# One kernel, one change: modulation sums streamed through the array, half a gate moved into the forgetting stage, and a memory projection taken token tile by token tile

## The chip, the cores and the metric

The kernel runs on one core of a Trainium2 chip. The number that counts is the device time of one execution, in microseconds. The kernel before took 1184.94 us (median of three runs, 1183.32 to 1185.14). The execution that was profiled took 1180.89 us, of which its trace spans 1179.1 us.

Names of the engines: PE is TensorE's matrix multiplication and PEld its weight load, DVE is VectorE, ACT is ScalarE, POOL is GpSimd, and SP is the queue that issues most DMAs.

## The reference

Two transformer blocks run one after the other on 512 tokens of 1024 channels. Only the first block's beginning matters here.

```python
mod = silu(c) @ w_ada + b_ada                     # c: 1024, w_ada: 1024 x 3072
shift, scale, gate = split(mod, 3)
h = rms_norm(x, g_pre) * (1 + scale) + shift
qa, ka, va, fa, za, qb, kb, vb, zb = split(h @ w_in, ...)
oa = forgetting_attention(qa, ka, va, fa + b_fgate) * silu(za)      # 8 heads of 64
ob = sliding_window_sink_attention(rope(qb), rope(kb), vb, sinks) * silu(zb)
x = x + gate * rms_norm(concat(oa, ob) @ w_out, g_post)
```

The second block reads a memory of 256 tokens, whose keys and values are `rms_norm(mem) @ w_mem_kv`.

## The kernel before

Most projections are done in a split form: a float32 matrix is cut into a high part (`wh`, `hh`) and a low rest (`wl`, `hl`), and three passes (high by high, high by low, low by high) replace one float32 product. A pass over 512 columns is one matmul. Weights come from memory as `raw` tiles (three buffers); ACT casts the high part, DVE or POOL subtracts for the low part.

**The opening.** `w_ada` for shift and scale is loaded in eight chunks of 1 MB (`load_ada`), five buffers in all. Chunk k gives shift and scale of channels 128k to 128k+127, as two columns. There are two ways to get them. `products(k, act)` and `products(k, dve)` scale the eight slices of the chunk by silu(c) and add them up on ACT and DVE, and `sums(k)` closes with two matmuls that have one column each. `sums_pe(k)` does the whole sum on PE with 16 matmuls of one column, the chunk itself being the stationary operand. Chunks 2, 3 and 5 go through `sums_pe`, the other five through `products`. Then `modulate(k)` adds the bias and `hidden(k)` forms `hh` and `hl` for the 128 channels: one ACT instruction, one on DVE or ACT, and a subtraction on POOL. At the end the `w1c` loop multiplies the eight channel tiles with a 264-column slice of `w_in` (keys and values of the window attention, forget gates): 12 matmuls for each k. All instructions in this part are in the order in which they are written, since `Ordered` pins them (line 345 is that helper, so all of them carry L345).

**Window attention and forgetting attention.** From here on the instructions are ordered by a list scheduler by priority, and what each engine gets is a fixed list. `staged` walks over attention steps in three phases (scores `sc`, transposes `tp`, product with values `pv`) and after each step calls `fill(k)`: the next k pieces of pending projection work, taken from a queue of generators. The window stage has two groups of four query blocks (`swa_sc`, `swa_tp`, `swa_pv`), two pieces for each step. Its queue holds the gates zb0, zb1, za0, za1 (`z_gen`: 48 matmuls each, two tanh, two DVE products) and the first query and key pair qk0. The forgetting stage has 32 steps (four head pairs `pr`, two heads, four query blocks) and one piece for each step. Its queue: `va`, `qk1`, `mv` (`value_row`), `qk2`, `qk3`, `gate` (`gate_row`). A step's scores need DVE to drain them, and there are two score banks, so PE can be two scores ahead of DVE.

`value_row` projects half of the memory's values: 256 tokens, that is two tiles t of 128, in two PSUM banks. For each of four weight quarters q it loads 512 KB of weights (`wv`, two buffers) and 256 KB of the transposed memory (`mT2`, one buffer), and runs 2 x 2 float32 matmuls:

```python
b = wk.tile([P, 2, 256], F32, tag="gb", name="mT2", bufs=1)
nc.sync.dma_start(out=b, in_=mT_d[:, 2 * q:2 * q + 2, :])
nc.sync.dma_start(out=a, in_=A["w_mem"][2][:, 2 * q:2 * q + 2, :])
```

SP issues DMAs in order, and one that waits for a buffer holds all behind it.

The functions that the change touches, with the lines that the profile names:

Of the kernel before, what the change touches and what calls it, by code (L numbers as in the profile page):

```python
# [20 lines left out]
P = 128  # L21
S = 512
NT = 4
KT = 8
# [16 lines left out]
NW = 512  # L41
# [51 lines left out]
def two_block_kernel(ctx: ExitStack, tc: tile.TileContext, A: dict, out: bass.AP):  # L93
    nc = tc.nc
    pe, act, dve, pool = nc.tensor, nc.scalar, nc.vector, nc.gpsimd
    fill = Fill()
# [49 lines left out]
    def mm_tile():  # L146
        return psm.tile([P, 512], F32, tag="mm", name="mm")
# [4 lines left out]
    def tp_tile():  # L152
        return pst.tile([P, 512], F32, tag="tp", name="tp")
# [210 lines left out]
    with ExitStack() as st:  # L364
# [8 lines left out]
        gs = pa1.tile([P, 8], F32, name="gs")  # L373
        mod = pa1.tile([P, 16], F32, name="mod")
# [18 lines left out]
        def squares(x, ss, ts):  # L393
            for t in ts:
                act.activation(out=xt[:, 2 * t:2 * t + 2, :].rearrange("p a b -> p (a b)"), in_=x[:, t, :], func=AF.Square, accum_out=ss[:, t:t + 1])
# [18 lines left out]
        def sums(k):  # L414
            pms[k] = tp_tile() if k in (0, 1, 4, 6) else mm_tile()
            for j in range(2):
                pe.matmul(out=pms[k][:, j:j + 1], lhsT=accs[k][0][:, j * P:(j + 1) * P], rhs=ones[:, 0:1], start=True, stop=True)

        def sums_pe(k):
            pms[k] = tp_tile() if k in (0, 1, 4, 6) else mm_tile()  # L420
            for j in range(2):
                for i in range(KT):
                    pe.matmul(out=pms[k][:, j:j + 1], lhsT=adas[k][:, i, j * P:(j + 1) * P], rhs=cs[:, i:i + 1], start=(i == 0), stop=(i == KT - 1))
# [43 lines left out]
        dve.tensor_copy(out=mrs, in_=rsqrt_small(pa, mss, 2, 1.0 / 1024, 1e-6, "rn2"))  # L467
        squares(xn, xss, range(NT))
# [11 lines left out]
        load_ada(5, 6, 7)  # L480
        sums(1)
        modulate(0)
        hidden(0, dve, pool)
        products(4, act)
        products(4, dve)
        sums_pe(3)
        sums(4)
        modulate(1)
        hidden(1, dve, pool)
        for t in range(2):  # L490
            act.activation(out=mk[:, t, :], in_=kb_[t], func=AF.Copy, scale=mrs[:, t:t + 1])
        modulate(2)
        hidden(2, dve, pool)
        products(6, act)
        products(6, dve)
        sums_pe(5)
        sums(6)
        wr, w = [], {}
        for q in range(4):
            wr.append(wp.tile([P, 2, 264], F32, tag="raw", name="raw", bufs=3))  # L500
            sp.dma_start(out=wr[q], in_=A["w1c"][:, 2 * q:2 * q + 2, :])
            if q == 2:
                break
# [9 lines left out]
        products(7, act)  # L513
        w1c_split(0, dve)
        wr.append(wp.tile([P, 2, 264], F32, tag="raw", name="raw", bufs=3))
        sp.dma_start(out=wr[3], in_=A["w1c"][:, 6:8, :])
        sp.dma_start(out=mT_d, in_=mT)
        modulate(3)
        hidden(3, act, pool)
        w1c_split(1, pool)  # L520
        modulate(4)
        hidden(4, act, pool)
        products(7, dve)
        w1c_split(2, dve)
        modulate(5)
        hidden(5, act, pool)
        w1c_split(3, dve)
        modulate(6)
        hidden(6, act, pool)
        wb = [sc_tile(), sc_tile(), pv_tile(), mm_tile()]  # L530
        for k in range(KT):
            if k == 4:
                sums(7)
                modulate(7)
                hidden(7, dve, dve)
            wh, wl = w[k]
            for t in range(NT):
                for i, (a, b) in enumerate(((hh, wh), (hh, wl), (hl, wh))):
                    pe.matmul(out=wb[t][:, 0:264], lhsT=a[:, k, t * P:(t + 1) * P], rhs=b, start=(k == 0 and i == 0), stop=(k == KT - 1 and i == 2))
# [95 lines left out]
    with ExitStack() as stS:  # L635
# [84 lines left out]
        fill.add("za1", z_gen("za1", 2))  # L720
# [77 lines left out]
        fill.until("za1")  # L798
# [27 lines left out]
    def value_row():  # L826

        banks = [mm_tile() for t in range(2)]
        for q in range(4):
            a = wk.tile([P, 2, NW], F32, tag="wg", name="wv")  # L830
            b = wk.tile([P, 2, 256], F32, tag="gb", name="mT2", bufs=1)
            nc.sync.dma_start(out=b, in_=mT_d[:, 2 * q:2 * q + 2, :])
            nc.sync.dma_start(out=a, in_=A["w_mem"][2][:, 2 * q:2 * q + 2, :])
            for k in range(2):
                for t in range(2):
                    m = pe.matmul(out=banks[t], lhsT=b[:, k, t * P:(t + 1) * P], rhs=a[:, k, :], start=(q + k == 0), stop=(2 * q + k == KT - 1))
                    if t == 0:
                        tie(m)
            if q < 3:
                yield  # L840
        mv = wk.tile([P, 2, NW], F32, tag="csb", name="mv2", bufs=1)
        for t in range(2):
            act.activation(out=mv[:, t, :], in_=banks[t], func=AF.Copy, scale=mrs[:, t:t + 1])
        nc.scalar.dma_start(out=v_d[:, :, 0:NW], in_=mv)
        yield
# [63 lines left out]
    fill.add("qk2", qk_gen(2, fa))  # L909
    fill.add("qk3", qk_gen(3, fb))  # L910
    fill.add("gate", gate_row())
    staged([(pr, m, n) for pr in range(4) for m in range(2) for n in range(NT)], fox_sc, fox_tp, fox_pv, 2, 1)
# [692 lines left out]
```

## Time and profile before

| | |
|---|---|
| median of three runs | 1184.94 us |
| profiled execution | 1180.89 us, span 1179.1 us |
| PE busy | 1151.2 us, 98% of the span |
| DVE busy | 877.5 us, 74% |
| ACT busy | 561.3 us, 48% |
| POOL busy | 194.1 us, 16% |
| moved by DMA | 168.39 MB, mean 143 GB/s |

PE is busy nearly always, so time is made of three things: the PE work there is, the clock at which it runs, and the few places where PE waits. The profile gives the first by its timeline, the second as a granted clock for any stretch (1.00 is full speed), the third as idle time with the releaser beside it.

### The profile page before, as it was taken

What the parts mean: (1) busy time and instruction counts of PE and PEld (TensorE: products, weight loads), DVE (VectorE), ACT (ScalarE), POOL (GpSimd) and SP (SyncE); (2) the same over time, 40 slices, a digit from 0 to 9 for tenths busy, and PEclk for the clock granted to TensorE, in tenths of its full rate; (3) what the DMA queues carried; (4) which work ended last, traced back from release to release, by engine and by line L of the source; (5) the groups of instructions that cost most, each with busy time, mean ns of one, the idle gap of its engine ahead of it and who ended that gap; (6) DMA issues with size and microseconds to landing.
All of it is one profiled execution on the core that took longest, in us unless ns stands there. A gap on an engine that the chain in (4) does not pass through costs nothing. (4 is left out here: it accounts for less than half of the span.)

```text
span 1179.1 us, 16340 instructions
## 1 busy us (share of the span) xinstructions
PE 1151.2 (98%) x5652; PEld 948.0 (80%) x5652; DVE 877.5 (74%) x1876; ACT 561.3 (48%) x1255; POOL 194.1 (16%) x153
## 2 busy tenths in 40 slices
PE   7999999999899999999999999999999999999998
PEld 4978777676688889888888778888888888888887
DVE  5786865666697599999999998999786287554342
ACT  6565754564564544555545544454433236232231
POOL 0441000000022202012020221031111031111000
PEclk9699999999999999999999999999999999999999
DMA  9643223455486332433334334343387455432233
GB/s 379 228 174 111 72 67 106 123 165 177 149 268 200 119 95 83 116 101 115 107 96 112 120 131 134 97 137 125 123 300 238 135 201 177 132 108 90 89 107 107
DMA packets 59905, 168.39 MB, mean 143 GB/s; under 512 B 7120, under 2 KB 10448, under 8 KB 58544
## 3 DMA queue, kind: packets, MB, share of 16 engines
q1 hardware_dynamic: 36544, 124.50, 33.5%
q10 hardware_dynamic: 23280, 42.86, 10.5%
q8 instruction: 44, 0.72, 0.3%
q14 instruction: 37, 0.30, 0.1%
HBM read 138.90 MB, written 21.63 MB: 136 GB/s over the span
## 5 line engine op out<-in xcount | busy, mean ns | idle before, releaser
L170 ACT CAST wh<-raw 128x512 fp32r<-128x512 f32 x352 | 212.6, 620 | 207.4 <-PE mm L202 101.6
L172 DVE TENSOR_TENSOR wl<-raw,wh 128x512 fp32r<-128x512 f32 x264 | 196.2, 755 | 99.7 <-ACT wh L170 98.0
L172 POOL TENSOR_TENSOR wl<-raw,wh 128x512 fp32r<-128x512 f32 x88 | 122.5, 1392 | 823.1 <-ACT wh L170 796.9
L202 PE MATMUL mm<-hh,wh 128*128 128x512 f32 x640 | 252.7, 395 | 0.0
L202 PE MATMUL mm<-hh,wl 128*128 128x512 f32 x640 | 251.3, 393 | 0.0
L202 PE MATMUL mm<-hl,wh 128*128 128x512 f32 x640 | 250.9, 392 | 0.0
L1052 DVE SCALAR_TENSOR_TENSOR cv<-u,vec,cv 128x512 f32<-128x512 f32 x240 | 192.8, 803 | 2.1
L202 PEld LDWEIGHTS mm<-hh,wl 128*128 128x128 f32 x640 | 120.2, 188 | 24.8 <-issue 0.2
L202 PEld LDWEIGHTS mm<-hh,wh 128*128 128x128 f32 x640 | 120.3, 188 | 23.5 <-issue 0.2
L202 PEld LDWEIGHTS mm<-hl,wh 128*128 128x128 f32 x640 | 120.4, 188 | 23.0
L221 PE MATMUL mm<-wh,hh 128*128 128x512 f32 x256 | 101.3, 396 | 0.0
L221 PE MATMUL mm<-wl,hh 128*128 128x512 f32 x256 | 100.9, 394 | 0.0
L221 PE MATMUL mm<-wh,hl 128*128 128x512 f32 x256 | 100.2, 393 | 0.0
L202 PE MATMUL mm<-bh,wh 128*128 128x512 f32 x192 | 75.2, 392 | 0.0
L202 PE MATMUL mm<-bh,wl 128*128 128x512 f32 x192 | 74.7, 389 | 0.0
L202 PE MATMUL mm<-bl,wh 128*128 128x512 f32 x192 | 74.7, 389 | 0.0
L1166 ACT ACTIVATE dp<-dp,dst 128x128 f32<-128x128 f32 (+3 forms) x64 | 35.8, 559 | 50.3 <-DVE dst L1164 49.0
L221 PEld LDWEIGHTS mm<-wh,hl 128*128 128x128 f32 x256 | 48.1, 188 | 9.7
L221 PEld LDWEIGHTS mm<-wh,hh 128*128 128x128 f32 x256 | 48.2, 188 | 9.2
L221 PEld LDWEIGHTS mm<-wl,hh 128*128 128x128 f32 x256 | 48.2, 188 | 8.7
L202 PEld LDWEIGHTS mm<-bl,wh 128*128 128x128 f32 x192 | 36.0, 188 | 7.7 <-issue 0.2
L202 PEld LDWEIGHTS mm<-bh,wh 128*128 128x128 f32 x192 | 36.0, 188 | 7.7 <-issue 0.2
(381 smaller groups left out, 2144.4 us busy)
## 6 DMA issues: line engine op xcount, KB each, us to landing
raw<-in_w_dram SPq DMA_DIRECT2D x88, 512.0 KB, 4.4
raw<-in_w_out_dram SPq DMA_DIRECT2D x24, 512.0 KB, 4.1
raw<-in_w2n_dram SPq DMA_DIRECT2D x24, 512.0 KB, 3.9
ada<-in_w_ada_dram SPq DMA_DIRECT2D x8, 1024.0 KB, 10.2
raw<-in_w1n_dram SPq DMA_DIRECT2D x8, 512.0 KB, 3.6
wg<-in_w_gate_dram SPq DMA_DIRECT2D x8, 512.0 KB
raw<-in_w_mem_dram SPq DMA_DIRECT2D x8, 512.0 KB, 4.3
k<-ks SPq DMA_DIRECT2D x32, 128.0 KB, 3.7
```

Of the source, the lines that this page charges most:

```text
L170: act.copy(out=wh, in_=raw[:, s])
L172: eng.tensor_tensor(out=wl, in0=raw[:, s], in1=f(wh), op=ALU.subtract)
L202: m = pe.matmul(out=ps, lhsT=a[:, c0:c0 + P], rhs=at(b, k), start=(n == 0 and i == 0), stop=(n == KT - 1 and i == 2))
L221: x = pe.matmul(out=ps, lhsT=at(a, k)[:, t * P:(t + 1) * P], rhs=b[:, 0:n], start=(m == 0 and i == 0), stop=(m == KT - 1 and i == 2))
L1052: dve.scalar_tensor_tensor(out=a, in0=u[:, j:j + S], scalar=dw[:, m * 31 + j:m * 31 + j + 1], in1=a, op0=ALU.mult, op1=ALU.add)
L1166: act.activation(out=p_[:, :w], in_=p_[:, :w], func=AF.Exp, scale=-1.0, bias=st_[:, 0, n, m:m + 1], accum_out=st_[:, 1, n, m:m + 1])
```

## The change

1. `sums_pe` no longer uses the chunk as stationary operand with a moving column. A new tile `csr` holds silu(c) repeated over 128 columns and is the stationary operand, and the chunk is streamed past it: 8 matmuls of 256 columns instead of 16 of one. Each row of the result is the same, and `column(k)` picks the diagonal with two fused DVE multiply-and-add instructions. Chunks 6 and 7 now go this way as well (their `products` are gone). The order of loads and of `modulate`/`hidden` is new, four `hidden` calls move a part from ACT to DVE, three move the subtraction from POOL to DVE, and chunks 6 and 7 are summed inside the `w1c` loop.
2. `za1` leaves the window stage's queue and joins the forgetting stage's, after `qk2`. The forgetting stage now takes alternately one and two pieces for each step.
3. `value_row` runs over token tiles on the outside: for each t one 512 KB tile of the transposed memory and all four weight quarters, so that the weights are loaded twice (2 MB more).

```diff
+        csr = pa1.tile([P, KT, P], F32, name="csr")
...
         def sums_pe(k):
-            pms[k] = tp_tile() if k in (0, 1, 4, 6) else mm_tile()
+
+            pms[k] = mm_tile()
+            for i in range(KT):
+                pe.matmul(out=pms[k][:, 0:256], lhsT=csr[:, i, :], rhs=adas[k][:, i, :], start=(i == 0), stop=(i == KT - 1))
+
+        def column(k):
+
+            row, pms[k] = pms[k], pa.tile([P, 2], F32, tag="colk", name="colk")
             for j in range(2):
-                for i in range(KT):
-                    pe.matmul(out=pms[k][:, j:j + 1], lhsT=adas[k][:, i, j * P:(j + 1) * P], rhs=cs[:, i:i + 1], start=(i == 0), stop=(i == KT - 1))
+                t = pa.tile([P, P], F32, tag="colt", name="colt", bufs=1)
+                dve.tensor_tensor_reduce(out=t, in0=row[:, j * P:(j + 1) * P], in1=ident, scale=1.0, scalar=0.0, op0=ALU.mult, op1=ALU.add, accum_out=pms[k][:, j:j + 1])
...
+        dve.tensor_copy(out=csr, in_=cs.unsqueeze(2).to_broadcast([P, KT, P]))
...
         sums(0)
         sums_pe(2)
-        load_ada(5, 6, 7)
         sums(1)
-        modulate(0)
-        hidden(0, dve, pool)
-        products(4, act)
-        products(4, dve)
         sums_pe(3)
-        sums(4)
-        modulate(1)
-        hidden(1, dve, pool)
...
+        load_ada(5)
...
+        for q in range(3):
+            w1c_load(q)
+        load_ada(6, 7)
+        modulate(0)
+        hidden(0, dve, pool)
+        column(2)
+        modulate(2)
+        hidden(2, dve, pool)
+        modulate(1)
+        hidden(1, dve, pool)
+        products(4, act)
+        products(4, dve)
+        sums(4)
+        column(3)
+        modulate(3)
+        hidden(3, dve, pool)
...
+        modulate(4)
+        sums_pe(5)
         w1c_split(0, dve)
+        hidden(4, dve, dve)
...
+        column(5)
+        modulate(5)
+        hidden(5, dve, dve)
...
         for k in range(KT):
-            if k == 4:
-                sums(7)
-                modulate(7)
-                hidden(7, dve, dve)
+            if k in (2, 3):
+                sums_pe(k + 4)
+                column(k + 4)
+                modulate(k + 4)
+                hidden(k + 4, dve, dve)
...
-        fill.add("za1", z_gen("za1", 2))
...
-        fill.until("za1")
+        fill.until("za0")
...
+        for t in range(2):
+            b = wk.tile([P, KT, P], F32, tag="csb", name="mT2", bufs=1)
+            nc.sync.dma_start(out=b, in_=mT_d[:, :, t * P:(t + 1) * P])
+            ps = mm_tile()
+            for q in range(4):
+                a = wk.tile([P, 2, NW], F32, tag="wg", name="wv")
+                nc.sync.dma_start(out=a, in_=A["w_mem"][2][:, 2 * q:2 * q + 2, :])
+                for k in range(2):
+                    m = pe.matmul(out=ps, lhsT=b[:, 2 * q + k, :], rhs=a[:, k, :], start=(q + k == 0), stop=(2 * q + k == KT - 1))
...
+    fill.add("za1", z_gen("za1", 2))
...
-    staged([(pr, m, n) for pr in range(4) for m in range(2) for n in range(NT)], fox_sc, fox_tp, fox_pv, 2, 1)
+    staged([(pr, m, n) for pr in range(4) for m in range(2) for n in range(NT)], fox_sc, fox_tp, fox_pv, 2, lambda i: 1 + i % 2)
```

**Place 1: DVE in the opening, from the first `ht` (channels 0) on.** `acc` are the products of chunk 4, `colt`/`colk` the new diagonal of chunk 2, `ht` the float32 form of a channel tile. Before:

```order
L345 TENSOR_SCALAR ht<-xt,gs,mod 128x512
L345 SCALAR_TENSOR_TENSOR acc<-ada,cs,acc 128x256 x6
L345 TENSOR_TENSOR acc<-acc 128x256
L345 SCALAR_TENSOR_TENSOR mod<-tp,vec 128x2
L345 SCALAR_TENSOR_TENSOR gs<-mod,vec 128x1
```

And with the change:

```order
L345 TENSOR_SCALAR ht<-xt,gs,mod 128x512
L345 ISA colt,colk<-mm,cst 128x128
L345 ISA colk 128x1
L345 ISA colt,colk<-mm,cst 128x128
L345 ISA colk 128x1
L345 SCALAR_TENSOR_TENSOR mod<-colk,vec 128x2
L345 SCALAR_TENSOR_TENSOR gs<-mod,vec 128x1
L345 TENSOR_SCALAR ht<-xt,gs,mod 128x512
L345 SCALAR_TENSOR_TENSOR mod<-tp,vec 128x2
L345 SCALAR_TENSOR_TENSOR gs<-mod,vec 128x1
L345 TENSOR_SCALAR ht<-xt,gs,mod 128x512
L345 SCALAR_TENSOR_TENSOR acc<-ada,cs,acc 128x256 x6
```

The products of chunk 4 now stand behind the diagonal of chunk 2 and two more channel tiles.

**Place 2: PE in the second group of the window stage.** `spt_1521` and `spt_1514` are the probabilities of its first query block, `sc_1639` and `sc_1604` scores of its second; `mm_1612` is the projection of za1. Before:

```order
L770 MATMUL tp_1670<-cst_79,spt_1521 128x128 x4
L747 MATMUL sc_1639<-kb11_973,qs_1499 128x256
L748 MATMUL sc_1639<-kbl1_974,qs_1499 128x256
L747 MATMUL sc_1644<-kb11_973,qs_1502 128x256
L748 MATMUL sc_1644<-kbl1_974,qs_1502 128x256
L202 MATMUL mm_1612<-hh_83,wh_1604 128x512
```

And with the change:

```order
L776 MATMUL tp_1630<-cst_79,spt_1514 128x128 x4
L753 MATMUL sc_1604<-kb11_966,qs_1495 128x256
L754 MATMUL sc_1604<-kbl1_967,qs_1495 128x256
L793 MATMUL pv_1669<-sph_1628,vbh_682 64x512
L753 MATMUL sc_1641<-kb11_966,qs_1481 128x256
L754 MATMUL sc_1641<-kbl1_967,qs_1481 128x256
L793 MATMUL pv_1669<-spl_1629,vbh_682 64x512
```

From there to the first score of the forgetting stage PE has attention alone, and no projection between the steps.

**Place 3: SP in the forgetting stage, around the memory's values.** `mT` are tiles of the transposed memory, `wv` weight quarters, `k_2233` and `k_2150` the first key tile of head pair 1, `q_2690` a query tile of head pair 3. Before:

```order
L627 DMA k_2233<-k_2233 64x512
L164 DMA raw<-in_w_out_dram 128x1024
L627 DMA k_2242<-k_2242 64x512
L832 DMA mT_2277<-mT_d 128x512
L833 DMA wv<-in_w_mem_dram 128x1024
```

And with the change:

```order
L634 DMA k_2150<-k_2150 64x512
L840 DMA wv<-in_w_mem_dram 128x1024
L164 DMA raw<-in_w_out_dram 128x1024
L634 DMA k_2159<-k_2159 64x512
L840 DMA wv<-in_w_mem_dram 128x1024 x2
L636 DMA q_2690<-aq_d 4x512
L637 DMA k_2691<-ak_d 4x512
L836 DMA mT_2249<-mT_d 128x8x128
L840 DMA wv<-in_w_mem_dram 128x1024
```

The second token tile's 512 KB `mT_2249` is one transfer into the one buffer that the first token tile has used to its last matmul.

## Rows read from the trace of the kernel before

**Rows 1.** The page's part 1: busy time and share of the span

```profile
PE 1151.2 (98%) x5652; PEld 948.0 (80%) x5652; DVE 877.5 (74%) x1876; ACT 561.3 (48%) x1255; POOL 194.1 (16%) x153
```

**Rows 2.** Stretches: length, each engine's busy us, granted clock, DMA share, GB/s

```profile
27.80:62.50 34.70, 34.51 (x214) 34.30 (x213) 26.45 (x54) 20.62 (x43) 12.24 (x10) 0.70 0.67 235
146.50:166.60 20.10, 19.82 (x108) 16.08 (x107) 16.21 (x55) 13.71 (x39) 2.63 (x2) 1.00 0.19 59
166.60:180.00 13.40, 11.27 (x53) 8.20 (x53) 6.56 (x22) 5.59 (x17) 0.00 (x0) 1.00 0.40 133
257.00:290.00 33.00, 32.00 (x132) 20.75 (x131) 23.09 (x70) 17.69 (x45) 2.42 (x2) 1.00 0.56 172
290.00:311.00 21.00, 15.30 (x85) 11.01 (x84) 12.19 (x30) 9.38 (x22) 0.14 (x1) 1.00 0.23 66
```

**Rows 3.** PE's timeline, opening: start, duration, instruction, idle before

```profile
9.92 14.36 PE L345 MATMUL sc<-rawm,mT 128*128 128x512 f32 x32
...
28.21 4.14 PE L345 MATMUL mm<-cs,ada 128*128 128x1 f32 x32
...
33.06 6.96 PE L345 MATMUL mm<-cs,ada 128*128 128x1 f32 x32
39.89 0.99 PE L345 MATMUL tp<-cst,acc 128*128 128x1 f32 x4
...
58.43 0.28 PE L345 MATMUL pv<-wh,hh 128*128 128x264 f32 x1
...
59.89 0.28 PE L345 MATMUL pv<-wh,hh 128*128 128x264 f32 x1
```

**Rows 4.** Half-microsecond stretches around the two changes of the granted clock

```profile
31.00:31.50 0.50, 0.50 (x6) 0.50 (x5) 0.50 (x2) 0.08 (x1) 0.00 (x0) 0.81 0.93 393
...
51.50:52.00 0.50, 0.50 (x5) 0.50 (x5) 0.00 (x0) 0.50 (x2) 0.04 (x1) 0.71 0.55 98
```

**Rows 5.** DVE's timeline, opening, and one fused instruction of the window stage

```profile
30.72 2.54 DVE L345 SCALAR_TENSOR_TENSOR acc<-ada,cs,acc 128x256 f32<-128x256 f32 x6 [1.33 <-ACT acc L345]
...
34.02 0.55 DVE L345 TENSOR_SCALAR ht<-xt,gs,mod 128x512 f32<-128x512 f32 x1
...
34.94 1.58 DVE L345 TENSOR_SCALAR ht<-xt,gs,mod 128x512 f32<-128x512 f32 x1
37.18 3.17 DVE L345 SCALAR_TENSOR_TENSOR acc<-ada,cs,acc 128x256 f32<-128x256 f32 x6 [0.65 <-ACT acc L345]
...
142.41 0.35 DVE L750 CUSTOM_DVE_ANT_0 spt<-sc,cst,nsink 128x128 f32<-128x128 f32 x1
```

**Rows 6.** POOL's timeline beside the slow `ht`

```profile
34.97 1.27 POOL L345 TENSOR_TENSOR hl<-ht,hh 128x512 fp32r<-128x512 f32 x1 [3.97 <-ACT hh L345]
```

**Rows 7.** DVE's groups by shape, 146.5 to 166.6: busy us, mean ns, idle

```profile
L750 DVE CUSTOM_DVE_ANT_0 spt<-sc,cst,nsink 128x256 f32<-128x256 f32 x12 | 5.4, 480 | 2.1 <-PE sc L748 2.1
L172 DVE TENSOR_TENSOR wl<-raw,wh 128x512 fp32r<-128x512 f32 x4 | 2.8, 691 | 1.7 <-ACT wh L170 1.7
...
L277 DVE SCALAR_TENSOR_TENSOR oz<-gt,mm 128x512 f32<-128x512 f32 x3 | 2.0, 670 | 0.0
```

**Rows 8.** The gates' matmuls (line 202) alone in one of these stretches: PE, PEld

```profile
146.50:166.60 20.10, 11.50 (x49) 8.70 (x48) 1.00 0.19 59
```

**Rows 9.** PE's timeline: the two waits after the window stage

```profile
175.53 0.44 PE L787 MATMUL pv<-sph,vbh 128*64 128x512 f32 x1 [0.35 <-ACT sph L772]
...
179.11 0.44 PE L859 MATMUL sc<-k,qs 128*128 128x384 f32 x1 [1.50 <-DVE fst L862]
```

**Rows 10.** PE's timeline where the memory's values begin

```profile
211.93 1.88 PE L836 MATMUL mm<-wv,mT 128*128 128x512 f32 x4
213.65 0.93 PE L875 MATMUL tp<-cst,fp 128*128 128x128 f32 x7
...
215.74 0.62 PE L859 MATMUL sc<-k,qs 128*128 128x128 f32 x1
```

**Rows 11.** The page's part 6: DMA issues, KB each, us from issue to landing

```profile
mT<-mT_d SPq DMA_DIRECT2D x4, 256.0 KB, 3.8
```

More of the change, by code (lines that the diff above doesn't have):

```diff
@@ L414, in sums @@
         def sums(k):
-            pms[k] = tp_tile() if k in (0, 1, 4, 6) else mm_tile()
+            pms[k] = tp_tile()
             for j in range(2):
@@ L419, in sums_pe @@
         def sums_pe(k):
-            pms[k] = tp_tile() if k in (0, 1, 4, 6) else mm_tile()
+            pms[k] = mm_tile()
[3 more added lines that the diff above has]
+            row, pms[k] = pms[k], pa.tile([P, 2], F32, tag="colk", name="colk")
             for j in range(2):
-                for i in range(KT):
-                    pe.matmul(out=pms[k][:, j:j + 1], lhsT=adas[k][:, i, j * P:(j + 1) * P], rhs=cs[:, i:i + 1], start=(i == 0), stop=(i == KT - 1))
+                t = pa.tile([P, P], F32, tag="colt", name="colt", bufs=1)
+                dve.tensor_tensor_reduce(out=t, in0=row[:, j * P:(j + 1) * P], in1=ident, scale=1.0, scalar=0.0, op0=ALU.mult, op1=ALU.add, accum_out=pms[k][:, j:j + 1])
         def modulate(k):
@@ L479, in two_block_kernel, with w1c_load @@
         sums_pe(2)
-        load_ada(5, 6, 7)
         sums(1)
-        modulate(0)
-        hidden(0, dve, pool)
-        products(4, act)
-        products(4, dve)
         sums_pe(3)
-        sums(4)
-        modulate(1)
-        hidden(1, dve, pool)
[L490 to L497, printed above, removed]
+        load_ada(5)
         wr, w = [], {}
-        for q in range(4):
+        def w1c_load(q):
             wr.append(wp.tile([P, 2, 264], F32, tag="raw", name="raw", bufs=3))
             sp.dma_start(out=wr[q], in_=A["w1c"][:, 2 * q:2 * q + 2, :])
-            if q == 2:
-                break
         def w1c_split(q, eng):
@@ L511, in w1c_split @@
                 w[2 * q + j] = (wh[:, 0, :], wl[:, 0, :])
-        products(7, act)
+        for q in range(3):
[15 more added lines that the diff above has]
+        for t in range(2):
+            act.activation(out=mk[:, t, :], in_=kb_[t], func=AF.Copy, scale=mrs[:, t:t + 1])
+        modulate(4)
+        sums_pe(5)
         w1c_split(0, dve)
-        wr.append(wp.tile([P, 2, 264], F32, tag="raw", name="raw", bufs=3))
-        sp.dma_start(out=wr[3], in_=A["w1c"][:, 6:8, :])
+        hidden(4, dve, dve)
+        w1c_split(1, pool)
+        w1c_load(3)
         sp.dma_start(out=mT_d, in_=mT)
[L518 to L523, printed above, removed]
+        column(5)
+        modulate(5)
+        hidden(5, dve, dve)
         w1c_split(2, dve)
-        modulate(5)
-        hidden(5, act, pool)
         w1c_split(3, dve)
-        modulate(6)
-        hidden(6, act, pool)
         wb = [sc_tile(), sc_tile(), pv_tile(), mm_tile()]
         for k in range(KT):
-            if k == 4:
-                sums(7)
-                modulate(7)
-                hidden(7, dve, dve)
+            if k in (2, 3):
[3 more added lines that the diff above has]
+                hidden(k + 4, dve, dve)
             wh, wl = w[k]
@@ L826, in value_row @@
     def value_row():
[L828 to L837, printed above, removed]
-                        tie(m)
[L839 to L845, printed above, removed]
+        for t in range(2):
+            b = wk.tile([P, KT, P], F32, tag="csb", name="mT2", bufs=1)
[6 more added lines that the diff above has]
+                    m = pe.matmul(out=ps, lhsT=b[:, 2 * q + k, :], rhs=a[:, k, :], start=(q + k == 0), stop=(2 * q + k == KT - 1))
+                    if k == 0:
+                        tie(m)
+                if q < 3:
+                    yield
+            mv = wk.tile([P, NW], F32, tag="gb", name="mv2", bufs=1)
+            act.activation(out=mv, in_=ps, func=AF.Copy, scale=mrs[:, t:t + 1])
+            nc.scalar.dma_start(out=v_d[:, t, 0:NW], in_=mv)
+            yield
     fxd = {}
```

## The prediction

> **What bounds the kernel now.** I read the page's busy shares first, then the busy time by stretches, then PE's timeline in the two stretches that the change edits, and last what DVE, ACT and SP do beside them. The shares say that PE is the bound: 1151.2 us busy out of 1179.1, DVE 74% [rows 1]. So a change pays by less PE work, a faster clock, or fewer PE waits, and costs by the opposite. The stretches show where there is anything to win or lose [rows 2]. From 27.8 to 62.5, the opening's sums and the 264-column projection, PE has no idle time but runs at a mean granted clock of 0.70. From 146.5 to 166.6, the second group of window attention, PE is busy 19.82 of 20.10 us and DVE 16.21: PE leads, with DVE not far behind. After that PE idles 2.1 us up to 180, 1.0 us from 257 to 290, and 5.7 us from 290 to 311, where the forgetting stage runs dry.
>
> **The opening.** The clock is 1.00 until about 31.3 and 0.50 until about 51.8 (a mean of 0.81 in the half microsecond from 31.0, of 0.71 in that from 51.5) [rows 4]; these are 2.4 and 1.2 GHz. What PE did before the fall was one-column matmuls, 16 for each chunk; before the rise it was 264-column matmuls. At the low level a chunk costs 39.89 - 33.06 = 6.83 us [rows 3]. A streamed chunk is not in the trace, but a float32 matmul of 512 columns is: 32 records (two for each matmul) in 14.36 us, 0.90 us each [rows 3]. Half the columns at half the price is 0.45 us, and eight of them 3.6 us, at full clock; a float32 stationary operand was hidden there too. The `w1c` loop at full clock takes 59.89 - 58.43 = 1.46 us for a channel tile [rows 3], 11.7 us for eight.
>
> Before, this stretch runs from 28.2 to 62.5, 34.3 us. After, at full clock, PE has five streamed chunks (18.0), two pairs of one-column sums (for chunks 1 and 4, 0.5 us each, half of the 0.99 that a pair takes at the low clock [rows 3]) and 11.7: 30.7 us, 3.6 less. But a wait comes in. PE's order is fixed: sums of chunk 1, streamed chunk 3, sums of chunk 4, streamed chunk 5. It reaches the sums of chunk 4 at 28.2 + 3.6 + 0.5 + 3.6 = 35.9. Their products stand on DVE behind the diagonal of chunk 2, which waits for PE until 31.8, and behind two `ht`. From 31.9: two fused instructions of 0.35 [rows 5], a pair of small ones, an `ht` of 0.55, another small pair, another `ht`, and then 3.3 us from the first product to the next `ht` (34.02 - 30.72) [rows 5]. With 0.4 for a small pair that is 31.9 + 0.7 + 0.4 + 0.55 + 0.4 + 0.55 + 3.3 = 37.8. Queued behind PE's wait are streamed chunk 5 and the whole `w1c` loop, so it counts fully: 1.9 us.
>
> It can be more. One `ht` took 1.58 us, not 0.55, and six products 3.17, not 2.54 [rows 5]; the first began as a POOL subtraction of 1.27 us did [rows 6]. The Trainium skill, page "SBUF — State Buffer", section "SBUF: two separate sides", says why: DVE and GpSimd share one pair of ports under an exclusive lock, and whichever starts first keeps it for the whole instruction while the other is blocked. The trace agrees, 1.58 us for 0.55. By that rule the second `ht` and the products meet the subtractions of channel tiles 2 and 1 again, since these follow right upon `hh`; without it they would not.
>
> With both slow values the wait is 1.9 + 1.0 + 0.6 = 3.5 us. The opening then gains between 1.7 and 0.1 us, if the clock holds. If the idle time costs the clock, a streamed chunk at the low level takes 3.6 us more, half a chunk 1.8. Bounds: -1.7 (the clock holds) to +1.8 (half a chunk lost, nothing gained); I take 0, the middle. The copy that makes `csr` and the diagonals of chunks 3, 5, 6, 7 lie on DVE beside PE work that lasts longer; if that cover were gone each diagonal would cost about 1.1 us (two times 0.35 and a small pair). The two chunks more that PE sums are counted; DVE and ACT lose two sets of products, which nobody waited for.
>
> **The window stage.** za1 takes 48 matmuls off the stretch 146.5 to 166.6. Line 202 has 49 there in 11.50 us [rows 8]; 48 are 11.3, in which the end of each run still overlaps its successor, so I use 11. That leaves 8.8 us of PE work. DVE loses two gate products of 0.67 and two or three weight subtractions of 0.69 [rows 7]: 16.2 less some 3.1 is 13.1. DVE is now the bound of this stretch. By its order all of this but the last two fused score instructions (0.45 us each by their group [rows 7]) comes before the low part of the second block's probabilities, for which PE waits: 12.2 us. Then PE has the product with the values and two blocks of transposes, about 2.2 us, to the first forgetting score. That is 14.4 us for 8.8 of PE work: 5.6 idle, against 0.3 in this stretch before [rows 2]. I take +5.0, a little under, because DVE's share of the stretch also holds some work that may slip behind it; bounds +3.5 (DVE's 13.1 alone, all PE work beside it but the last transposes) and +6.5 (the round trips to ACT for the row sums not hidden).
>
> **The forgetting stage.** Its PE work grows by the same 11 us that the window stage lost; this is neither gain nor loss. First piece: after the last window block PE waits for `pv` (0.35 and 0.28) and for DVE's first forgetting score (1.50) [rows 9]. Eight matmuls now stand ahead of that `pv`, so the first two go: -0.6. The 1.50 stays; DVE still has those scores behind the window stage's last product.
>
> Second piece, the memory's values. They come right after qk1. Before, the key tile of head pair 1 made its way from PE's last key matmul (211.9) over ACT and a DMA to the score at 215.74: 3.8 us [rows 10], filled with four value matmuls of two token tiles, 0.9 each, and seven transposes. Now two such matmuls (1.8) and seven transposes (0.9) stand in front of that score: 1.1 us short. Then the second token tile. Its `mT` load may start only when the first tile's last matmul is done; until its own first matmul PE has two score pairs, seven transposes and one more score, about 2.0 us. A load of half its size took 3.8 us to land [rows 11], so 1.8 or more is short. On PE the second half of qk2 and everything else stands behind it. Sum 2.9, taken as +3.0; bounds 0 (DVE, slow there with eight steps in a row, makes PE wait anyway in the same place) and +5.
>
> Third piece, the end. Pieces come one and two at a time, so the queue empties earlier, but it holds za1 more. The waits of 1.0 and 5.7 us [rows 2] could shrink by 2.1 at most (the rest is the last step's own chain) or grow by as much, when the gate's weight matmuls are used up and DVE must still make the high and low parts of the attention outputs. I take -0.5.
>
> **Sum.** 0 + 5.0 - 0.6 + 3.0 - 0.5 = +6.9 us. On the profiled execution, 1180.9, that is 1187.8. The median of the runs before is 4.05 us above it, so the forecast for the median is 1191.8, rounded to 1192.
>
> **Rivals.** *The forgetting stage takes up what the window stage loses.* The opening keeps its clock and gains 1.7, the window stage costs 3.5, the values 1.0 (the key only), -0.6 and -1.0 elsewhere: +1.2, 1186.1, no change. For it: DVE has slack there, 23.1 of 33 us [rows 2]. Against it: PE was hardly idle in that stage, so there is little to soak up. *The clock pays.* The wait for chunk 4 stays away, because ACT and DVE run ahead of these sums: 3.6 us gained in full; then window stage +3.5, end -2.1, pieces one and two -0.6 and 0: -2.8, 1182.1, faster. It decides from the point at which chunk 4's products end before 35.9. Against it: the order of place 1, in which they cannot start before 34.5. *The clock stays low.* If PE's idle time brings the low clock and it lasts over three streamed chunks, 3 x 3.6 = 10.8 us are added to the forecast's opening: about 1201 with a gain of 1.7 taken off. For it: the fall at 31.3 lasted 20 us. Against it: streamed chunks are dense columns, like the memory projection at 9.9, which ran at full clock.
>
> **How the numbers follow.** Differences under 0.2% (2.4 us) can't be told from no change here. Forecast 0.66 with a range of its own of 1188 to 1196; no change 0.17; faster 0.11; the low clock 0.06. The first and last are slower, less 0.01 for its lower edge and the second's edges: slower 0.72, same 0.17, faster 0.11. The bounds of the terms add up to -1.7 + 3.5 - 0.6 + 0 - 2.1 = -0.9 and 1.8 + 6.5 + 5 + 2 - 0.6 = +14.7; all at one end is not likely, so 1184 to 1198.
>
> **What would show it.** Right: the clock at 1.00 through most of the opening, a PE wait of 2 to 4 us at the sums of chunk 4, the projection's end within 2 us of 62.5, some 5 us of PE idle time in the second window group with DVE busy throughout, and waits of PE for the key tile and for `mT` among the value matmuls. Wrong: no wait in the opening, or a window group in which PE idles under 3 us, or no wait at the second token tile.

## The result, and the profile after

The changed kernel takes 1194.44 us, median of four runs (1193.51 to 1197.86), against 1184.13 for the kernel before beside it (1181.32 to 1185.14): 10.3 us more, a ratio of 1.0095 with a 95% interval of 1.0077 to 1.0114. The forecast was 1192.0, with a range of 1184 to 1198 and slower as the likeliest side.

The profiled execution of the changed kernel took 1197.86 us (span 1196.1), the longest of its four; the profiled one of before (1180.89, span 1179.1) was a short one. The two spans differ by 17.0 us, so the question is first which part of that is the change. I cut both traces at the same three places: the first matmul of line 221 behind the `w1c` projection, the first score of the forgetting stage, and PE's restart of the output projection behind its wait for `ohl`. First the three stretches of the changed kernel (busy us with counts of PE, PEld, DVE, ACT, POOL; granted clock; DMA share; GB/s), then those of the kernel before:

```profile
64.90:162.70 97.80, 93.97 (x459) 74.41 (x458) 76.88 (x223) 60.36 (x153) 20.73 (x27) 1.00 0.31 94
162.70:324.00 161.30, 147.78 (x666) 108.45 (x664) 88.24 (x239) 75.28 (x180) 8.99 (x7) 0.98 0.42 128
324.00:1196.10 872.10, 859.38 (x4239) 721.60 (x4239) 668.60 (x1293) 386.08 (x842) 152.88 (x105) 1.00 0.43 139
```

```profile
62.50:166.60 104.10, 102.74 (x508) 82.90 (x506) 82.14 (x232) 65.23 (x163) 22.28 (x28) 1.00 0.34 105
166.60:310.10 143.50, 134.55 (x616) 97.33 (x615) 85.65 (x237) 72.44 (x174) 7.78 (x6) 1.00 0.41 125
310.10:1179.10 869.00, 857.81 (x4239) 720.48 (x4239) 667.92 (x1293) 384.47 (x842) 151.57 (x105) 1.00 0.44 139
```

The last stretch is the same work in both (4239 matmul records), and 3.1 us longer. In the other kernels below it takes from 868.5 to 872.0, and its length follows none of the change's parts, so I put those 3 us down to the execution. What is left is 13.9 us. The medians differ by only 10.3, so some 3.6 us of the 13.9 then belong to these two executions as well; with one trace of each kernel it is not shown which. By stage, and with "loses" for what goes beyond the moved work: the opening ends 2.4 later; the window stage is 6.3 shorter, though some 11.3 us of matmuls left it, so it loses 5.0; the forgetting stage is 17.8 longer, of which 11.3 came with za1, so it loses 6.5.

**The opening**, answering to [rows 3]. PE's timeline (start, duration, instruction, and in brackets the idle time before it and what ended it):

```profile
28.40 3.70 PE L345 MATMUL mm<-ada,csr 128*128 128x256 f32 x16
...
39.69 0.98 PE L345 MATMUL tp<-cst,acc 128*128 128x1 f32 x4 [3.69 <-DVE acc L345]
40.54 6.08 PE L345 MATMUL mm<-ada,csr 128*128 128x256 f32 x16
...
49.35 3.61 PE L345 MATMUL mm<-ada,csr 128*128 128x256 f32 x16
```

A streamed chunk takes about 3.6 us, as worked out (3.70 by its records, 3.54 to its successor); PE waits 3.69 us for chunk 4's products, and chunk 5 behind the wait takes 6.08. DVE in that time, then POOL, answering to [rows 5, 6]:

```profile
34.19 1.52 DVE L345 TENSOR_SCALAR ht<-xt,gs,mod 128x512 f32<-128x512 f32 x1
35.63 3.46 DVE L345 SCALAR_TENSOR_TENSOR acc<-ada,cs,acc 128x256 f32<-128x256 f32 x6
```

```profile
34.15 1.28 POOL L345 TENSOR_TENSOR hl<-ht,hh 128x512 fp32r<-128x512 f32 x1 [2.96 <-DVE gs L345]
35.85 1.37 POOL L345 TENSOR_TENSOR hl<-ht,hh 128x512 fp32r<-128x512 f32 x1 [0.43 <-ACT acc L345]
```

`ht` and the products begin as the two POOL subtractions do and are slow, 1.52 us for 0.55 and 3.46 for 2.54. (The rule of the Trainium skill, page "SBUF — State Buffer", section "SBUF: two separate sides", that I put beside the sum says that whichever of DVE and GpSimd starts first keeps the shared ports for its whole instruction; the trace agrees, with these numbers.) The granted clock around the wait and behind it (length, PE busy, clock, DMA share, GB/s), answering to [rows 4]:

```profile
35.00:40.00 5.00, 1.30 (x7) 0.85 0.68 288
38.50:45.50 7.00, 5.81 (x16) 0.51 0.13 26
40.00:50.00 10.00, 10.00 (x48) 0.73 0.51 185
50.00:62.00 12.00, 12.00 (x78) 1.00 0.56 177
```

So the old fall at 31.3 is gone, and a new one comes within the idle time: the clock is low from about 38.5 to 45.2.

**The window stage.** Its second group, answering to the second of [rows 2], cut 2.4 us later, as the opening ended:

```profile
148.90:162.70 13.80, 11.07 (x58) 7.42 (x57) 12.84 (x50) 10.54 (x35) 1.30 (x1) 1.00 0.14 40
```

DVE is busy 12.84 of 13.80 us; it was 16.21 of 20.10. PE's busy share hides part of the loss: it does 8.8 us of work by the sum and shows 11.07, since a matmul that stands alone shows its whole length (a score of 256 columns 0.39 us here, 0.28 in a chain).

**The forgetting stage**, answering to [rows 9 to 11]. PE's timeline again, rows with waits and two others; behind them the granted clock after the longest and near the stage's end, and SP's issue of the second token tile's `mT`:

```profile
176.85 0.45 PE L864 MATMUL sc<-k,qs 128*128 128x384 f32 x1 [1.50 <-DVE fst L867]
...
210.65 0.30 PE L864 MATMUL sc<-k,qs 128*128 128x128 f32 x1 [1.03 <-ACT pth L882]
...
217.90 1.88 PE L842 MATMUL mm<-wv,mT 128*128 128x512 f32 x4
...
225.13 2.63 PE L842 MATMUL mm<-wv,mT 128*128 128x512 f32 x4 [3.49 <-DMA mT<-mT_d]
226.77 1.42 PE L202 MATMUL mm<-hh,wh 128*128 128x512 f32 x1
...
252.11 0.30 PE L864 MATMUL sc<-k,qs 128*128 128x128 f32 x1 [1.59 <-DMA k<-k]
...
284.05 1.98 PE L819 MATMUL mm<-wg,csb 128*128 128x512 f32 x4 [1.41 <-DMA wg<-in_w_gate_dram]
```

```profile
225.00:230.00 5.00, 4.87 (x11) 0.66 0.37 109
316.00:324.00 8.00, 4.64 (x19) 0.79 0.00 0
```

```profile
219.81 0.57 SPq L836 DMA_DIRECT2D mT<-mT_d  x1
```

The load is issued when the first tile's last products (217.90) are done, and PE goes on 5.3 us after its issue, at 225.13; the trace gives 4.5 from issue to landing. Then five microseconds at a clock of 0.66 cost 1.7 more. A second low stretch comes near the stage's end, 0.79 from 316 to 324, behind waits of 0.97, 0.68 and 0.17 us. The kernel before waits about as long in that place and ran at 1.00, so this fall may be the execution's. Over the stage PE idles 161.3 - 147.8 = 13.5 us against 143.5 - 134.6 = 8.9 before, and its busy time is 147.8 against 134.6 + 11.3: 4.6 us of waits and 1.9 of longer busy time, which holds both low stretches, make up the 6.5.

### The profile page after: what moved, and what is told of

Its sections match the earlier page's. It is cut to its first block, busy times and chain, and to the rows that moved or that the text cites. A ratio compares the mean times of both kernels' runs of the same rounds, so it can differ in the third digit from the quotient of the medians.

```text
span 1196.1 us, 16314 instructions
## 1 busy us (share of the span) xinstructions
PE 1156.1 (97%) x5628; PEld 947.7 (79%) x5628; DVE 874.6 (73%) x1890; ACT 558.4 (47%) x1247; POOL 191.5 (16%) x150
## 4 chain that ended last, share of the span: by engine, by line
PE 73%; DVE 18%; DMA 5%; issue 2%; ACT 2%; POOL 0%; SPq 0%; ACTq 0%; DVEq 0%
PE mm L202 42%; PE mm L221 14%; DVE cv L1058 5%; DVE wl L172 3%; PE mm L213 2%; PE mm L345 2%; PE sc L345 2%; DVE dp L1170 1%; PE pv L903 1%; PE mm L842 1%; DMA raw<-in_w_out_dram 1%; PE sc L1322 1%; PE pv L1365 1%; PE tp L295 1%; DMA wg<-in_w_gate_dram 1%
## 5 line engine op out<-in xcount | busy, mean ns | idle before, releaser
L172 DVE TENSOR_TENSOR wl<-raw,wh 128x512 fp32r<-128x512 f32 x264 | 193.3, 743 | 97.3 <-ACT wh L170 95.7
L202 PE MATMUL mm<-hh,wh 128*128 128x512 f32 x640 | 255.7, 399 | 0.0
```

What stands on the lines that cost most here:

```text
L172: eng.tensor_tensor(out=wl, in0=raw[:, s], in1=f(wh), op=ALU.subtract)
L202: m = pe.matmul(out=ps, lhsT=a[:, c0:c0 + P], rhs=at(b, k), start=(n == 0 and i == 0), stop=(n == KT - 1 and i == 2))
```

## The experiments

The twelve kernels of this section were timed beside the kernel before, whose median was 1183.57, 1182.99, 1182.45 and 1183.99 in the four sets. The ratios are made from all runs of a set and can differ by 0.1% from the quotient of its medians. Stage lengths are cut at the places named above, from one profile each.

```
kernel                     median   ratio to before, 95%     opening  window  forgetting  rest
before                     -        -                        62.5     104.1   143.5       869.0
changed                    1194.44  1.0095 [1.0077, 1.0114]  64.9      97.8   161.3       872.1
opening_alone              1184.68  1.0008 [0.9995, 1.0020]  65.7     103.9   142.8       870.7
za1_alone                  1189.35  1.0044 [1.0027, 1.0061]  63.1      98.1   154.3       872.0
value_alone                1190.57  1.0069 [1.0048, 1.0091]  63.2     104.1   151.4       869.2
halves_loaded              1188.45  1.0039 [1.0024, 1.0055]  66.0      97.8   157.5       868.6
opening_no_wait            1182.36  0.9991 [0.9977, 1.0004]  63.4     103.8   142.5       870.9
za1_even_window            1185.67  1.0019 [1.0006, 1.0031]  63.1      97.4   152.1       870.9
za1_even_both              1181.41  0.9979 [0.9964, 0.9994]  62.3      97.5   148.4       870.1
value_long_pieces          1190.32  1.0060 [1.0039, 1.0081]  62.6     104.1   151.1       868.9
change_even                1191.49  1.0080 [1.0063, 1.0098]  64.9      97.4   158.1       869.9
change_even_halves         1184.73  1.0019 [1.0007, 1.0031]  65.1      97.4   151.4       869.1
opening_streamed_za1_even  1179.36  0.9978 [0.9965, 0.9990]  62.2      96.8   148.7       868.5
change_mended              1181.73  0.9981 [0.9968, 0.9993]  60.6      97.5   151.5       870.9
```

### The three parts, each alone

**opening_alone**: the change's part 1; in the other two places the lines of before.

> The kernel before with the change's opening alone (modulation chunks 2, 3, 5, 6, 7 streamed; za1 and the value half as before). Theory A, from the milestones of the two profiles: the end of the w1c projection came 2.4 us later (64.93 against 62.53 us), because the sums of chunk 4 waited 3.69 us and chunk 5 then ran at the low clock; so +2.4 us, 1186.5 against 1184.1. Theory B, the prediction's own sum: the wait and the higher clock cancel, 0 (1184.1). Theory C, the clock pays once the stages behind it are as before: -2, 1182. A wait of 3 to 4 us at the sums of chunk 4 is to be seen under every one of them.

The wait is there (3.69 us, `acc`) and the projection ends 3.1 us later than before, yet the time is +1.1 us and its interval (-0.6 to +2.4) holds theory B's 0 as well as A's 2.4. In the traces the change's opening ends at 64.9 to 66.0 in five kernels and the old one at 62.3 to 63.2 in six, so it does come late. But the opening is not where the 10 us come from.

**za1_alone**: before, with

```
-        fill.add("za1", z_gen("za1", 2))          (window stage)
...
-        fill.until("za1")
+        fill.until("za0")
...
+    fill.add("za1", z_gen("za1", 2))              (forgetting stage, ahead of qk3)
...
-    staged(..., fox_sc, fox_tp, fox_pv, 2, 1)
+    staged(..., fox_sc, fox_tp, fox_pv, 2, lambda i: 1 + i % 2)
```

> The kernel before with za1 queued in the forgetting stage and its fill of 1 or 2 pieces a step; opening and value half as before. Theory A: the window stage loses 5 us more than the 11.5 us of matmuls that left (VectorE sets its pace and TensorE waits), and the forgetting stage does not give this back: +5 to +6.5 us, 1189 to 1190.6. Theory B, rival (a) of the prediction: the forgetting stage takes the pieces into its own waits, 0 to +1.5, 1184 to 1185.6.

Theory A: +5.8 us by the medians. The window stage loses 5.3 (98.1 for 104.1 - 11.3), and the forgetting stage, 10.8 longer with 11.3 us more work, gives back 0.5.

**value_alone**: before, with `value_row` of the change.

> The kernel before with the value half projected token tile by token tile; opening and za1 as before. Theory A: the second token tile's half of the memory can be loaded only when the first tile's last product is done; TensorE then waits about 3.5 us for it and loses some 1.5 us more to the low clock behind it: +3.5 to +5 us, 1187.6 to 1189. Theory B: that wait is TensorE's only because za1's move changed what is queued there; in the old queue other pieces cover it: 0 to +1, 1184 to 1185.

+7.0 us by the medians, more than either theory. The forgetting stage is 7.9 longer. PE's waits that are new in it (`pth` is the high part of the transposed probabilities):

```profile
216.18 0.30 PE L858 MATMUL sc<-k,qs 128*128 128x128 f32 x1 [0.97 <-ACT pth L876]
230.29 2.40 PE L836 MATMUL mm<-wv,mT 128*128 128x512 f32 x4 [3.16 <-DMA mT<-mT_d]
257.19 0.30 PE L858 MATMUL sc<-k,qs 128*128 128x128 f32 x1 [1.53 <-ACT pth L876]
```

The wait for `mT` is A's. The two for `pth` are not in the sum: a piece is now two products instead of four, and one piece a step is taken here. The three parts alone add up to 13.9 us, more than the whole change. Its filler of one and two pieces in turn covers some of these: it has one wait for `pth` at the scores, and change_even below, at one piece a step, has two again.

### What the value half pays for

**halves_loaded**: the changed kernel, with

```
-            b = wk.tile([P, KT, P], F32, tag="csb", name="mT2", bufs=1)
-            nc.sync.dma_start(out=b, in_=mT_d[:, :, t * P:(t + 1) * P])
+            b = [wk.tile([P, 4, P], F32, tag=f"csb{h}", name="mT2", bufs=1) for h in range(2)]
+            nc.sync.dma_start(out=b[0], in_=mT_d[:, 0:4, t * P:(t + 1) * P])
...
+                if q == 0:
+                    nc.sync.dma_start(out=b[1], in_=mT_d[:, 4:8, t * P:(t + 1) * P])
...
```

> The changed kernel, with the transposed memory of the value half held in two tiles of four k-slices each, so that the second token tile's first half is loaded while the first tile's last four products still run (the gate's constant is split the same way). Theory A: the wait of 3.5 us and the low clock behind it go, -3.5 to -5 us against the changed kernel, 1189.5 to 1191. Theory B: the steps of the forgetting stage, which stood still during that wait, need the time in any case, or the wait moves to the weights wv behind it: -1 to 0, 1193.4 to 1194.4.

Theory A by the time, and a little more: 6.0 us less than the changed kernel. No wait for `mT` is left; one of 0.69 us for `wv` stands in its place. The low clock did not go in this trace, it moved (0.57 from 282 to 286), and the stage is only 3.8 shorter:

```profile
221.45 1.96 PE L845 MATMUL mm<-wv,mT 128*128 128x512 f32 x4 [0.69 <-DMA wv<-in_w_mem_dram]
```

```profile
282.00:286.00 4.00, 4.00 (x10) 1.90 (x8) 1.54 (x6) 0.60 (x2) 0.00 (x0) 0.57 0.34 93
```

That the low clock can go with the wait is to be seen in the trace of change_even_halves below.

**value_long_pieces**: value_alone with

```
-                if q < 3:
+                if q == 1:
                     yield
```

> The value half alone, token tile by token tile (as in value_alone), with four products in a piece, as before the change, in place of two. Theory A: of the 7 to 8 us that the value half cost by itself, 3.2 us are the wait for the second half of the memory and 2.5 us are two waits for pth, since pieces of two products no longer cover a step; with long pieces the latter go: -2 to -3 against 1190.57, 1187.5 to 1188.5, and the wait for mT stays at 3 to 4 us. Theory B: the waits for pth come from the extra loads or from where the pieces fall in the queue: within 1 us of 1190.57.

Theory B by the time. The waits for `pth` (2.5 us) do go, but another wait comes in their place, 1.38 us for `wv`:

```profile
218.20 1.98 PE L836 MATMUL mm<-wv,mT 128*128 128x512 f32 x4 [1.38 <-DMA wv<-in_w_mem_dram]
...
230.21 3.64 PE L836 MATMUL mm<-wv,mT 128*128 128x512 f32 x4 [3.34 <-DMA mT<-mT_d]
```

The weights are loaded twice now, through two buffers: eight loads of 512 KB where four were enough before. Longer pieces reach the next ones before they have landed. The rest is the clock: it falls near the end of the stage in this trace (0.57 from 311.7 to 315.7) and does not in that of value_alone.

### What za1's move pays for

**za1_even_window**: za1_alone with `swa_sc, swa_tp, swa_pv, 1, 1` for `1, 2`.

> za1 alone in the forgetting stage (as in za1_alone), and one piece of filler at each step of the window stage in place of two. 12 pieces are left there for 12 calls; with two at a step they end about halfway. Theory A: the 5.5 us that the window stage lost come from its tail, where no piece is left while VectorE paces it, and not from VectorE's total work (over the stage it is busy some 80%): spread out, they cover the tail, the stage (w1c's end to the first forgetting score) takes 93 to 95 us against 98.1, and the kernel 3 to 5 us less than za1 alone (1189.35): 1184.5 to 1186.5. Theory B, the prediction's: VectorE bounds the stage once za1 is gone; the waits only move forward, and the time stays within 1 us of 1189.35.

The time is A's, 3.7 us less than za1_alone, but not at A's place: the window stage takes 97.4 us for 98.1. The waits moved forward to where DVE makes the second group's queries, and the clock fell behind the longer one:

```profile
134.34 0.33 PE L746 MATMUL sc<-kb,qs 128*128 128x128 f32 x1 [1.61 <-DVE qs L288]
```

```profile
135.00:139.00 4.00, 4.00 (x18) 0.58 0.00 0
```

So moving the pieces does not shorten the window stage, as theory B and the prediction have it. The low clock is not the reason: opening_streamed_za1_even below has the same pieces and the same wait of 1.61 us, its clock stays at 1.00, and its stage takes 96.8:

```profile
62.20:159.00 96.80, 93.21 (x461) 74.07 (x460) 78.49 (x231) 61.50 (x157) 19.26 (x26) 1.00 0.29 85
```

Nearly all of PE's waits in the stage are for VectorE. Yet VectorE is busy only 78.5 of these 96.8 us, so I take it that the places at which PE needs it count, and not its total; no run moves VectorE's work to show it. 2.2 us of the gain came in the forgetting stage; za1_alone ran at 0.81 of the clock from 305 to 313 there, this kernel at 1.00. Why, with that stage's pieces the same, I did not settle. Since the same wait was followed by a fall here and by none in opening_streamed_za1_even, it may be the execution.

**za1_even_both**: also `fox_sc, fox_tp, fox_pv, 2, 1`.

> The same with one piece at each step of the forgetting stage too (the change takes 1 and 2 in turn), where 36 pieces then stand against 35 steps. Theory A: the 8.3 us that TensorE idles in that stage lie for the most part at its end, after the last piece, and at full steps none; even, the last steps are covered: another 2 to 4 us less than the run before it. Theory B: the waits of the last steps go to the steps in the middle, or to the gate's products, which are then late for the output projection: the same time within 1 us, or 1 to 3 us more.

Theory A: 4.3 us less again. The ratio is 0.2% under before, with an interval just clear of 1; the medians are 1.6 us apart. That is at the limit which the prediction set for telling a change from none. The forgetting stage:

```profile
159.80:308.20 148.40, 143.28 (x663) 106.18 (x661) 88.32 (x232) 74.62 (x175) 10.64 (x8) 1.00 0.43 131
```

PE idles 5.1 us in it, against 8.3 in za1_alone and 8.9 before: 36 pieces for 35 calls (32 steps, and three more until the last step is through) last to the end. At one and two in turn the calls asked for 52 and used them up early. With pieces that last, the stage does take up part of za1's work: 148.4 us for 143.5 + 11.3.

**change_even** and **change_even_halves**: both fills at one piece, in the changed kernel and in halves_loaded.

> The changed kernel with one piece of filler a step in the window stage (two before) and one a step in the forgetting stage (one and two in turn before). Theory A: what za1 alone gained by this (1189.35 to 1185.67 to 1181.41, 8 us) is gained here too, since pieces then last to the end of both stages; the wait of 3.5 us for the memory's second half stays: 1186 to 1188. Theory B: with 40 pieces against 35 steps the forgetting stage has filler to spare as it is, so that only the window's 3.7 us come back: 1190 to 1191.

> The same, and the memory's second half loaded in two tiles as in halves_loaded. Theory A: the causes are separate and add up: 1194.4 - 8 (even pieces) - 6 (halves, 1194.4 to 1188.45) = 1180.4, 1179 to 1182, so that the change with both mended is no slower than before. Theory B: both cover the same idle time of the forgetting stage; the halves then bring 2 us or less beside the even pieces, 1184 to 1187.

The first is theory B: 3 us, not 8; the wait of 3.60 us for `mT` and two for `pth` (2.5) are left:

```profile
224.30 3.75 PE L842 MATMUL mm<-wv,mT 128*128 128x512 f32 x4 [3.60 <-DMA mT<-mT_d]
```

The second lies in B's range, but not for B's reason: the halves bring 6.8 us, as they did before; it was the even pieces that brought less. In its trace neither the wait for `mT` nor a low clock is left in the stage, which takes 151.4 us for 158.1.

### The opening, and the parts together

**opening_no_wait**: opening_alone with chunk 3's diagonal and the first `w1c` split ahead of `products(4, ...)`, and

```
+            if k == 1:
+                sums(4)
+                modulate(4)
+                hidden(4, dve, dve)
```

> The change's opening alone, with chunk 3's scale and the first w1c split ahead of chunk 4's products on VectorE, and the sums of chunk 4 behind the first k-step of the w1c projection on TensorE, so that TensorE does not wait 3.7 us for them. Theory A: the wait goes, and chunk 5 and the first w1c products run at full clock; the projection ends near 59 to 60 us (62.53 before, 65.65 with the opening alone), and the kernel takes 2.5 to 3.5 us less than before: about 1181 against 1183.6 to 1184. Theory B: the first w1c products wait for their split halves or hl instead, the projection ends at 62 or later, and the time is that of before within 1 us.

Theory B by its numbers, with another wait: the projection ends at 63.4, the time is 0.6 us under before, inside the interval. The wait shrank to 1.80 us and a new one of 1.27 came, for the bank that ACT reads `mk` from; the clock fell behind them (0.50 from 45 to 47).

**opening_streamed_za1_even**: za1_even_both with the change's opening and

```
         sums_pe(3)
+        sums_pe(4)
...
-        products(4, act)
-        products(4, dve)
-        sums(4)
         column(3)
...
+        column(4)
         modulate(4)
```

> The parts that pay, together: the opening with chunk 4 streamed on TensorE too (right behind chunk 3, so that VectorE has no products of chunk 4 and TensorE nothing to wait for), za1 in the forgetting stage, one piece a step in both stages, the value half as before the change. Theory A: TensorE streams chunks 2 to 5 without a gap from 28.2 to 42.9 us at full clock and the w1c projection ends at 61 to 62 us (62.5 before, 63.4 in opening_no_wait); with za1 even in both stages at 1181.4 that gives about 1180, 0.996 to 0.998 of before. Theory B: the 3.6 us of products that TensorE takes on weigh as much as the wait that goes, the projection ends at 63 or later, and the time is that of za1_even_both, 1181 to 1182.

Theory A for the opening; the stretch from 28.00, answering to the first of [rows 2], and PE in it:

```profile
28.00:62.10 34.10, 34.10 (x210) 31.55 (x209) 22.02 (x70) 18.34 (x41) 8.59 (x8) 1.00 0.74 274
```

```profile
33.25 10.61 PE L345 MATMUL mm<-ada,csr 128*128 128x256 f32 x48
```

Three chunks in a row, no wait, full clock; it ends at 62.2 though its sums began at 28.98, 1.0 us later than in the changed kernel. From the first sums to its end it takes 33.2 us for 34.7 before. The kernel takes 0.9978 of before, as za1_even_both does (0.9979), whose opening ends at 62.3: that the opening adds to the gain over before is likely from the trace, and not shown by the times.

**change_mended**: change_even_halves with this opening and pieces of four products.

> The whole change with its costs mended: chunk 4 streamed on TensorE as in opening_streamed_za1_even, one piece a step in both stages, the memory's halves loaded as in change_even_halves, and pieces of four products in the value half in place of two. Theory A: against change_even_halves (1184.73) the opening gives 3 us, and the 2.3 us that TensorE still waits for pth among the value half's short pieces go: 1179 to 1180, level with opening_streamed_za1_even (1179.36), so that the value half in two token tiles costs nothing by itself. Theory B: as in value_long_pieces, a wait for the weights wv, now loaded twice, takes the place of the waits for pth: 1181 to 1182.5, and the value half in this form is worth leaving out.

Theory B: the forgetting stage takes 151.5 us, as in change_even_halves (151.4) and 2.8 more than with the old value half, and PE waits for `wv` again:

```profile
208.43 1.99 PE L844 MATMUL mm<-wv,mT 128*128 128x512 f32 x4 [1.71 <-DMA wv<-in_w_mem_dram]
...
216.01 1.96 PE L844 MATMUL mm<-wv,mT 128*128 128x512 f32 x4 [0.49 <-DMA wv<-in_w_mem_dram]
```

Against the change's own opening the streamed one does show: of the stages only the opening is shorter than in change_even_halves (60.6 for 65.1), and the kernel takes 3.0 us less, with intervals that do not meet. All three parts, mended, take 0.9981 of before, again with an interval just clear of 1. That the value half is better left out is the trace's word; the two ratios overlap.

## Why the prediction was right, point by point

The side and the size came out (+10.3 us for +7.9), with one term right, two too small, and some luck in the medians.

- **The window stage, +5.0.** Measured 5.0 by the traces, and 5.3 in za1_alone. The reason holds too: DVE is busy 12.84 of 13.80 us in the second group, and moving the pieces (za1_even_window) could not shorten the stage. Only the sign that I named, 5 us of idle PE, was the wrong one to look for: PE shows 2.7 idle in the group, under my own bound of 3, because lone matmuls show longer.
- **The opening, 0 with a bound of +1.8.** The wait was sized well (3.5 with both slow values; 3.69 measured). The step that failed is the clock behind it: I allowed half a chunk at the low level, 1.8; most of one ran so (6.08 for 3.70, +2.4), and the sums ahead of it too (+0.5). The projection ended 2.4 us late, not within 2. That is outside the bound of +1.8. In the time of opening_alone this is +1.1 and hardly to be told from nothing.
- **The forgetting stage, +1.9.** The first piece is right: `pv` no longer waits, the 1.50 stays. The second, +3.0, is the mis-sized term. The wait at the first value products came at its size, 1.03 for 1.1, but by luck: it is for `pth` and not for the key tile. That for `mT` was 3.49 against 1.8: I took 3.8 us to land from a load of half the size [rows 11], and it was 4.5 to land and 5.3 from its issue to PE's next product. The low clock behind it, 1.7 us, was not in the sum at all; nor were the low stretch at the stage's end, 1.59 us for a key of a later head pair and 1.75 for the gate's weights (0.5 before). The last is not the value half's doing, since za1_alone waits 1.8 there too; the key's is gone in change_even, where the filler comes evenly. The wait for `mT` and the low clock together are 6.8 us between change_even and change_even_halves; between the changed kernel and halves_loaded, where the low clock only moved, the medians give 6.0 and the stage 3.8.
- **The rivals.** That the forgetting stage takes up the window's loss fell with za1_alone: 0.5 us given back. With pieces that last to its end (za1_even_both) it gives back 6.4, so it was the filler's pace, and not the stage, that stood against this rival. That the clock pays fell with the wait. The low clock lasted over most of one chunk, not three.
- **The sum against the runs.** The traces give +13.9 where I had +6.9, with some 3.6 of the 13.9 from the executions, and the medians give +10.3. The forecast starts from the median of before, 4.05 us above its profiled execution, which was a short one, while that of the changed kernel was a long one; so it came nearer than the sum came to the traces. The sum itself was 3.4 us short of the medians. That the forecast missed by only 2.4 is in part luck: its median of before, 1184.94, lay 0.8 above the one beside the result.

What slowed the kernel is thus shown for two of its parts: za1's move (5 to 6 us) and the value half's load (6 to 7 us). With pieces that last to the end of each stage, an earlier load and no wait in the opening the same change takes 0.2% less than before, and without the value half as well; both intervals are only just clear of 1.

## What to carry to other kernels

Filler work is worth what it covers in its last piece: count the pieces and the calls, and let them end together; here that, in both stages, turned za1's move from +0.4% to -0.2%. A wait on the leading engine is to be priced with the granted clock that may come behind it: 3.5 us of waiting cost 5.2 in the one place, and 3.7 cost 6.6 in the other. A loop order that reloads an operand needs a buffer for the load to start in; without one the way from the last use to the landing is a wait, less what else the engine has to do (here 3.49 of the 5.3 us).

## What the runs showed of the hardware

With one-column matmuls for the streamed chunks PE was busy 34.51 of 34.70 us in the opening and was granted 0.70 of the clock [rows 2]; with 256-column matmuls in their place (opening_streamed_za1_even), 34.10 of 34.10 busy, it was granted 1.00. A busy PE in the records is therefore not yet one at full clock.

Nor does the same wait always bring the same fall. Behind 1.61 us of waiting for `qs` in the window stage the clock was 0.58 from 135 to 139 in za1_even_window; behind 1.61 us at the same matmul it stayed at 1.00 in opening_streamed_za1_even:

```profile
133.44 0.33 PE L752 MATMUL sc<-kb,qs 128*128 128x128 f32 x1 [1.61 <-DVE qs L288]
```

```profile
134.00:138.00 4.00, 4.00 (x25) 3.50 (x25) 3.26 (x12) 3.10 (x11) 0.00 (x0) 1.00 0.01 4
```
